# Gating copies of the modulation loads moved from VectorE to GpSimd, and the first feed-forward weight split ordered behind the second norm

## The chip, the core and the metric

One NeuronCore of a Trainium2 chip runs the whole program. TensorE (PE in the rows, PEld for its weight loads), VectorE (DVE), ScalarE (ACT), GpSimd (POOL) and SyncE (SP, which only issues transfers here) each work through a queue of their own in a fixed order and wait for one another by semaphores. The metric is device microseconds of one execution; less is better.

## What is computed

A decoder block over 256 tokens of width 2048: two parallel branches (attention over 8 heads, and a diagonal state-space scan), merged by gates, then a gated feed-forward layer with a short causal convolution. Both sub-layers are normalised and modulated by vectors that a conditioning vector `c` gives through `w_mod`. What matters here is the second half:

```
mod = silu(c) @ w_mod + b_mod
sh1, sc1, g1, sh2, sc2, g2 = split(mod, 6)
...
merged = sigmoid(gate_a) * (y_attn @ w_attn_br) + sigmoid(gate_s) * (y_ssm @ w_ssm_br)
x  = x + g1 * (merged @ w_out)
h2 = rms_norm(x, norm2_g) * (1 + sc2) + sh2
up = causal_dwconv(h2 @ w_up, conv_w, conv_b)
val, gt = split(up, 2)
x  = x + g2 * ((silu(gt) * val) @ w_down)
```

## The kernel before

All weights are float32 and are streamed once, in pieces of 128 x 1024 (512 KB), through a ring of five buffers named `raw`. A piece is split in two: ScalarE rounds it to a high part `whi` (L186), VectorE subtracts that from the piece to get the low part `wlo` (L191). TensorE then multiplies with both parts (L302, L304 for most stages, L268 to L272 for the first feed-forward block). `whi` and `wlo` have three buffers each, so the splits run two to three pieces ahead of TensorE. A `raw` buffer is free again when its piece has been split.

The stages follow each other as `glup` (the gate of the scan branch), `ppp` (its output projection), `outp` (`w_out`), the second norm, then pairs of `gp` and `vp` (the two halves of `w_up`) and `dp` (`w_down`).

Modulation weights come in between. From the stage `glup` on they have a ring of their own, four buffers named `mraw`. There are two kinds. For the gates g1 and g2, 64 pieces (`in_w_g_dram`) are each multiplied with `cb`, which is silu(c) on all partitions, and summed along the row by one VectorE instruction (L493, "gate product" below). For the last quarter of sh2, eight pieces (`in_w_m_dram`) are multiplied on TensorE (L456, tile `modp`), copied to `rows` (L463), transposed (`modt`, L478) and reduced on VectorE (L479). These eight stand at the second norm.

All loads of weights are issued by SP in one queue, so a load that waits holds back those behind it. Loads of modulation weights would run far ahead of the work if only a free buffer held them. Line 122 holds them back: ahead of the load it copies one element of the newest `wlo` into the first element of the `mraw` buffer. The load, which writes the same buffer, must wait for the copy, and the copy waits for the split and for the buffer.

The second norm works in these steps. `add_to` (L329) adds the last two rows blocks into `x`. ScalarE squares them (L528). TensorE sums the squares over the partitions (`sqs`, L533). In `norm_rows`, VectorE copies the sums (L547), TensorE adds them up (`pv`, L550), VectorE makes `v` (L551), runs ten tiny instructions for the inverse root (L396 to L400), writes two diagonal tiles `dg` (L558), TensorE spreads these over the partitions (`pr`, L559), and VectorE copies the result to `rb` (L560). `modulate` then needs `rb`: L567 makes `t`, ScalarE makes the high part of `hl` (L571), VectorE the low part (L572). The first `gp` matmul needs the first `hl`.

The instructions of each engine are put in order when the program is built, by a scheduler that follows estimated times and may move an instruction ahead of others that stand before it in the code. So the first three splits of `w_up` may land among the steps of the norm, although the code makes them behind it.

GpSimd has little to do from the stage `glup` on: it issues the load of `cb` (L505) and four loads of `x` (L1220).

Of the kernel before, what the change touches and what calls it, by code (L numbers as in the profile page):

```python
# [10 lines left out]
F32 = mybir.dt.float32  # L11
# [31 lines left out]
def block_kernel(ctx: ExitStack, tc: tile.TileContext, I, out):  # L43
    nc = tc.nc
    V, A, PE, DMA = nc.vector, nc.scalar, nc.tensor, nc.sync
# [15 lines left out]
    def py_tile(shape, name):  # L61
        return ps.tile(shape, F32, name=name, tag="py", bufs=1)
# [20 lines left out]
    def w4(name, shape, dt=F32):  # L83
        if int(np.prod(shape[1:])) > 512:
            return post.tile(list(shape), dt, name=name, tag="w8", bufs=2)
        return sm.tile(list(shape), dt, name=name, tag="w4", bufs=2)
# [17 lines left out]
    loaded = []  # L104
    place = {"load": 0}
# [6 lines left out]
    def ring_of(i):  # L112
        return "mod" if plan[i][0] == "m" and "mod" in ring else "w"

    def load_next():
        kind, src, _ = plan[place["load"]]
        r = ring_of(place["load"])
        held[r] += 1
        raw = ring[r]()

        if r == "mod" and "lo" in place:
            V.tensor_copy(raw[:, 0, 0:1], place["lo"][:, 0, 0:1].bitcast(F32))
        flat = raw.rearrange("p a b -> p (a b)")
        DMA.dma_start(flat, src)
        loaded.append((raw, r))
        place["load"] += 1

    behind = {}

    def after(inst, earlier):  # L130

        tc.add_manual_dep(inst.ins, earlier.ins.name,
                          mybir.DependencyInfo(mybir.DependencyClass.NoSync, mybir.DependencyReason.DATA),
                          reason="order")
# [5 lines left out]
    def unload(i):  # L140
        held[loaded[i][1]] -= 1
        loaded[i] = None

    def load_ahead():
        while place["load"] < len(plan):
            r = ring_of(place["load"])
            if held[r] >= room[r]:
                break
            load_next()

    def load_until(i):
        while place["load"] <= i and place["load"] < len(plan):
            load_next()
# [28 lines left out]
    hi_lo = {}  # L182
# [5 lines left out]

    def split_lo(i):
        lo = wp.tile([128, 2, 512], F32R, name="wlo", tag="wlo", bufs=WB)  # L190
        V.tensor_sub(lo, loaded[i][0], hi_lo[i][0].bitcast(F32))  # L191
        hi_lo[i][1] = lo
        place["lo"] = lo
        unload(i)
# [11 lines left out]
    def split_ahead(n):  # L206
        while done["hi"] <= n + WB - 1 and done["hi"] < len(weights):
            load_until(weights[done["hi"]])
            split_hi(weights[done["hi"]])
            split_lo(weights[done["hi"]])  # L210
            done["hi"] += 1
# [22 lines left out]
    def flush():  # L234
        while agenda:
            clock["step"] = min(agenda)
            for f in agenda.pop(clock["step"]):
                f()
# [156 lines left out]
    def rsqrt(y, v, t):  # L395
        V.tensor_scalar(y.bitcast(I32), v.bitcast(I32), -0.5, 1597463007.0, op0=ALU.mult, op1=ALU.add)  # L396
        for _ in range(3):
            V.scalar_tensor_tensor(t, y, -0.5, y, op0=ALU.mult, op1=ALU.mult)
            V.tensor_mul(t, t, v)
            V.scalar_tensor_tensor(y, t, 1.5, y, op0=ALU.add, op1=ALU.mult)  # L400
# [120 lines left out]
    rb = const.tile([128, 256], F32, name="rb")  # L521
# [19 lines left out]
    def norm_rows(st, after=None):  # L541

        v2 = sm.tile([128, 2], F32, name="v2", tag="v2", bufs=1)
        r2 = sm.tile([128, 2], F32, name="r2", tag="r2", bufs=1)
        t2 = sm.tile([128, 2], F32, name="t2", tag="t2", bufs=1)
        sqs = w4("sqs", (128, 256))
        V.tensor_copy(sqs, st["p"])  # L547
        pv = py_tile([128, 2], "pv")
        for t in range(2):
            PE.matmul(pv[:, t:t + 1], sqs[:, 128 * t:128 * t + 128], ones[:, 0:1], start=True, stop=True)  # L550
        V.tensor_scalar(v2, pv, 1.0 / (32 * D), EPS, op0=ALU.mult, op1=ALU.add)  # L551
        rsqrt(r2, v2, t2)
        pr = py_tile([128, 256], "pr")
        dg = w4("dg", (128, 2, 128))
        if after is not None:
            V.tensor_copy(dg[:, 0, 0:1], after)
        for t in range(2):
            V.tensor_scalar(dg[:, t], ident, r2[:, t:t + 1], None, op0=ALU.mult)  # L558
            PE.matmul(pr[:, 128 * t:128 * t + 128], ones, dg[:, t], start=True, stop=True)  # L559
        V.tensor_copy(rb, pr)  # L560

    def modulate(c, src, a, sh):

# [455 lines left out]
    for q in range(8):  # L1019
        squares(st1, range(2 * q, 2 * q + 2), xT[q])  # L1020
    norm_rows(st1, a1[:, 0:1])
    mods += m0[len(m0) // 2:]
    all_mods()
# [217 lines left out]
    st2 = {}  # L1241
# [11 lines left out]
    all_mods()  # L1253
    go()
    flush()
    norm_rows(st2)
    mods += late
    all_mods()
    go()
# [149 lines left out]
```

## Time and profile before

| | |
|---|---|
| median of three runs | 1552.86 us (1548.08 to 1556.23) |
| the profiled execution's own time | 1551.37 us |
| its span, first to last instruction | 1549.6 us |
| PE busy in the span | 1491.3 us (96%) |
| VectorE busy | 1052.7 us (68%) |
| ScalarE busy | 847.4 us (55%) |
| GpSimd busy | 11.3 us (1%), 25 instructions |
| mean granted TensorE clock | 0.992 |
| bytes moved | 354.54 MB, 229 GB/s on average |

Line numbers are those of the kernel before. An interval in brackets in a row is the idle time of that engine just ahead of the instruction, with what ended it by the profile. The rows of matmuls overlap each other, since they are pipelined. All times within the execution count from the start of the span.

### The profile page before, as it was taken

To read this page: it belongs to the slowest core of one execution; us is meant where nothing else is said; L and a number is where in the kernel's file an instruction comes from. 1 tells how busy PE (TensorE), PEld (TensorE's weight loads), DVE (VectorE), ACT (ScalarE), POOL (GpSimd) and SP (SyncE) were. 2 spreads that over 40 slices of the span, in tenths; PEclk is the share of its full clock that TensorE was granted. 3 is DMA by queue.
4 is the path that set the end of the run, shared out by engine and by line. 5 is a ranking of instruction groups with operands and counts; after the bars stand their busy time and mean duration, and the time that the engine had idled before them with its cause. 6 is when DMAs were issued, how large, how long until landed. Compare 5 with 4: busy or idle time off the path is not lost.

```text
span 1549.6 us, 24718 instructions
## 1 busy us (share of the span) xinstructions
PE 1491.3 (96%) x9624; PEld 1239.2 (80%) x9624; DVE 1052.7 (68%) x1778; ACT 847.4 (55%) x1201; POOL 11.3 (1%) x25
## 2 busy tenths in 40 slices
PE   6999989999999999899989999999999999999998
PEld 3656757689886678788869888888888888888887
DVE  2787443786774567799769888887555576666654
ACT  3766656967674543654435555555444455555442
POOL 1000000000000000000000000000000000000000
PEclk9999999999999999999999999999999999999999
DMA  8887777643348776879877777776555555565663
GB/s 308 282 311 279 251 269 255 233 166 121 124 150 284 276 251 209 294 255 345 309 254 241 247 247 257 243 252 207 190 191 190 190 187 190 191 189 189 203 210 111
DMA packets 99252, 354.54 MB, mean 229 GB/s; under 512 B 10976, under 2 KB 13152, under 8 KB 99008
## 3 DMA queue, kind: packets, MB, share of 16 engines
q1 hardware_dynamic: 97808, 348.17, 65.5%
q0 software_dynamic: 1184, 4.66, 0.8%
q8 instruction: 75, 1.23, 0.3%
q14 instruction: 41, 0.34, 0.1%
q10 hardware_dynamic: 144, 0.14, 0.0%
HBM read 350.83 MB, written 2.10 MB: 228 GB/s over the span
## 4 chain that ended last, share of the span: by engine, by line
PE 78%; DVE 8%; DMA 8%; ACT 5%; issue 2%; SPq 0%; ACTq 0%; DVEq 0%; POOLq 0%
PE vp L302 10%; PE dp L302 10%; PE gp L302 10%; PE dp L304 5%; PE vp L304 5%; PE gp L304 5%; DMA raw<-in_w_in_dram 3%; PE outp L302 3%; DVE wlo L191 3%; PE modp L456 3%; PE gap L302 3%; ACT whi L186 2%; PE ppp L302 2%; PE outp L304 2%; PE gap L304 2%
## 5 line engine op out<-in xcount | busy, mean ns | idle before, releaser
L191 DVE TENSOR_TENSOR wlo<-raw,whi 128x1024 fp32r<-128x1024 f32 x464 | 566.8, 1224 | 404.4 <-ACT whi L186 401.9
L186 ACT CAST whi<-raw 128x1024 fp32r<-128x1024 f32 x464 | 486.7, 1050 | 562.3 <-PE dp L302 131.9
L302 PE MATMUL vp<-hl,whi 128*128 128x512 f32 x704 | 247.2, 395 | 0.5 <-DVE gate L1272 0.5
L302 PE MATMUL dp<-g,whi 128*128 128x512 f32 x704 | 244.5, 391 | 0.0
L302 PE MATMUL gp<-hl,whi 128*128 128x512 f32 x640 | 224.5, 395 | 0.0
L304 PE MATMUL dp<-g,wlo 128*128 128x256 f32 x704 | 197.8, 281 | 0.0
L304 PE MATMUL vp<-hl,wlo 128*128 128x256 f32 x704 | 197.4, 280 | 0.0
L304 PE MATMUL gp<-hl,wlo 128*128 128x256 f32 x640 | 179.5, 280 | 0.0
L302 PEld LDWEIGHTS vp<-hl,whi 128*128 128x128 f32 x704 | 132.0, 188 | 31.8 <-issue 0.8
L302 PEld LDWEIGHTS dp<-g,whi 128*128 128x128 f32 x704 | 131.9, 187 | 28.7
L302 PEld LDWEIGHTS gp<-hl,whi 128*128 128x128 f32 x640 | 120.0, 187 | 28.1
L304 PEld LDWEIGHTS dp<-g,wlo 128*128 128x128 f32 x704 | 133.0, 189 | 0.0
L304 PEld LDWEIGHTS vp<-hl,wlo 128*128 128x128 f32 x704 | 133.0, 189 | 0.0
L304 PEld LDWEIGHTS gp<-hl,wlo 128*128 128x128 f32 x640 | 120.9, 189 | 0.0
L302 PE MATMUL gap<-hl,whi 128*128 128x512 f32 x256 | 93.9, 406 | 0.6 <-ACT whi L186 0.5
L302 PE MATMUL outp<-m,whi 128*128 128x512 f32 x256 | 91.2, 400 | 0.2 <-DVE m L1155 0.2
L493 DVE SCALAR_TENSOR_TENSOR mraw<-mraw,cb 128x1024 f32<-128x1024 f32 x64 | 77.8, 1220 | 16.1 <-DMA mraw<-in_w_g_dram 9.2
L456 PE MATMUL modp<-raw,cpad 128*32 128x512 f32 (+1 forms) x544 | 75.2, 561 | 6.0 <-DMA raw<-in_w_m_dram 3.6
L304 PE MATMUL gap<-hl,wlo 128*128 128x256 f32 x256 | 72.9, 285 | 1.1 <-DVE wlo L191 0.9
L304 PE MATMUL outp<-m,wlo 128*128 128x256 f32 x256 | 71.7, 281 | 0.2 <-DVE wlo L191 0.2
L302 PEld LDWEIGHTS gap<-hl,whi 128*128 128x128 f32 x256 | 48.1, 188 | 20.6 <-ACT whi L186 4.2
L302 PEld LDWEIGHTS outp<-m,whi 128*128 128x128 f32 x256 | 48.0, 188 | 14.4 <-issue 2.5
(339 smaller groups left out, 2554.5 us busy)
## 6 DMA issues: line engine op xcount, KB each, us to landing
raw<-in_w_up_dram SPq DMA_DIRECT2D x176, 512.0 KB, 4.3
raw<-in_w_m_dram SPq DMA_DIRECT2D x120, 512.0 KB, 5.2
raw<-in_w_in_dram SPq DMA_DIRECT2D x96, 512.0 KB, 4.8
raw<-in_w_down_dram SPq DMA_DIRECT2D x88, 512.0 KB, 3.5
mraw<-in_w_g_dram SPq DMA_DIRECT2D x64, 512.0 KB, 5.0
raw<-in_w_ga_dram SPq DMA_DIRECT2D x32, 512.0 KB, 3.9
raw<-in_w_out_dram SPq DMA_DIRECT2D x32, 512.0 KB, 5.6
raw<-in_w_attn_br_dram SPq DMA_DIRECT2D x16, 512.0 KB, 4.8
```

The costliest lines, as they stand in the source:

```text
L186: A.copy(hi, loaded[i][0])
L191: V.tensor_sub(lo, loaded[i][0], hi_lo[i][0].bitcast(F32))
L302: follow(PE.matmul(joined(p[m]), hi4[:, k, ms], joined(a), start=u == 0 and k == 0, stop=False, skip_group_check=True))
L304: PE.matmul(p[m][:, 0], lo4[:, k, ms], a[:, 0], start=False, stop=u == kbs - 1 and k == 3, skip_group_check=True)
L456: mm = PE.matmul(st["p"][r0:r0 + 32], cpad[:, k], raw[:, i], start=k < 4, stop=k >= 12, tile_position=(0, r0))
L493: V.scalar_tensor_tensor(flat, flat, 1.0, cb[:, 1024 * half:1024 * half + 1024], op0=ALU.mult, op1=ALU.mult, accum_out=sums[:, k, half:hal ...
```

## The change

The copy of line 122 is issued on GpSimd in place of VectorE. It copies the same element, and the load waits for it as before. `norm_rows` hands back its last instruction, the copy to `rb`, and the first `wlo` split that the code makes after the second norm may not stand ahead of that copy on VectorE. This is an order only, without a semaphore.

```
@@ load_next
         if r == "mod" and "lo" in place:
-            V.tensor_copy(raw[:, 0, 0:1], place["lo"][:, 0, 0:1].bitcast(F32))
+            nc.gpsimd.tensor_copy(raw[:, 0, 0:1], place["lo"][:, 0, 0:1].bitcast(F32))
@@ split_lo
-        V.tensor_sub(lo, loaded[i][0], hi_lo[i][0].bitcast(F32))
+        split = V.tensor_sub(lo, loaded[i][0], hi_lo[i][0].bitcast(F32))
+        if "norm" in behind:
+            after(split, behind.pop("norm"))
@@ norm_rows
-        V.tensor_copy(rb, pr)
+        return V.tensor_copy(rb, pr)
@@ behind the stage outp
-    norm_rows(st2)
+    behind["norm"] = norm_rows(st2)
```

The scheduler's order changes with it, on VectorE, TensorE, ScalarE and SP, and only between the stage `glup` and the end of the gate products. In the changed kernel the line numbers behind the second edit are two higher. Three places follow.

VectorE at the start of the second norm, in the kernel before (`v` and `r` are the steps of the inverse root):

```order
L547 COPY sqs<-sqs 128x256
L122 COPY mraw<-wlo 128x1 x2
L551 TENSOR_SCALAR v_7874<-pv 128x2
L122 COPY mraw<-wlo 128x1 x2
L396 TENSOR_SCALAR r_7875<-v_7874 128x2
L191 TENSOR_TENSOR wlo<-raw,whi 128x1024
L398 SCALAR_TENSOR_TENSOR t_7876<-r_7875 128x2
```

The same place in the changed kernel:

```order
L549 COPY sqs<-sqs 128x256
L553 TENSOR_SCALAR v_7874<-pv 128x2
L398 TENSOR_SCALAR r_7875<-v_7874 128x2
L400 SCALAR_TENSOR_TENSOR t_7876<-r_7875 128x2
L401 TENSOR_TENSOR t_7876<-t_7876,v_7874 128x2
```

The four copies and the split between the steps are gone. The end of the same norm on VectorE, before:

```order
L558 TENSOR_SCALAR dg<-p_73,r_7875 128x128 x2
L560 COPY rb<-pr 128x256
L122 COPY mraw<-wlo 128x1 x2
L567 SCALAR_TENSOR_TENSOR t<-x_6697,a_103,rb 128x256 x3
L572 SCALAR_TENSOR_TENSOR hl<-t,sh_102,hl 128x256 x2
```

And in the changed kernel:

```order
L560 TENSOR_SCALAR dg<-p_73,r_7875 128x128 x2
L562 COPY rb<-pr 128x256
L191 TENSOR_TENSOR wlo<-raw,whi 128x1024 x3
L569 SCALAR_TENSOR_TENSOR t<-x_6697,a_103,rb 128x256 x3
L574 SCALAR_TENSOR_TENSOR hl<-t,sh_102,hl 128x256
```

Two copies have left, and three splits now stand between `rb` and the first `t`: the one shown above, and two that stood ahead of the last `add_to` before. TensorE through the norm, before:

```order
L533 MATMUL sqs<-sq,ones 32x256 x2
L456 MATMUL modp<-mraw,cpad 32x512 x4
L550 MATMUL pv<-ones,sqs 128x1 x2
L456 MATMUL modp<-mraw,cpad 32x512 x4
L559 MATMUL pr<-dg,ones 128x128 x2
L456 MATMUL modp<-mraw,cpad 32x512 x7
L268 MATMUL gp<-hl,whi 128x256
```

And in the changed kernel:

```order
L458 MATMUL modp<-mraw,cpad 32x512 x4
L552 MATMUL pv<-ones,sqs 128x1 x2
L458 MATMUL modp<-mraw,cpad 32x512 x3
L561 MATMUL pr<-dg,ones 128x128 x2
L458 MATMUL modp<-mraw,cpad 32x512 x8
L270 MATMUL gp<-hl,whi 128x256
L480 MATMUL modt<-p_73,rows 128x128 x4
```

One `modp` product, the first of the fifth piece, has moved from ahead of `pr` to behind it, and the transposes `modt` now follow the first `gp` matmul, where six stood ahead of them before. The last place is VectorE late in the stage `outp`, where pieces 21 to 23 of `w_out` are split, before:

```order
L191 TENSOR_TENSOR wlo<-raw,whi 128x1024
L493 SCALAR_TENSOR_TENSOR mraw,gsum<-mraw,cb 128x1024
L122 COPY mraw<-wlo 128x1
L493 SCALAR_TENSOR_TENSOR mraw,gsum<-mraw,cb 128x1024
L191 TENSOR_TENSOR wlo<-raw,whi 128x1024
L319 TENSOR_TENSOR ts<-ts,outp 128x512
L493 SCALAR_TENSOR_TENSOR mraw,gsum<-mraw,cb 128x1024
L329 SCALAR_TENSOR_TENSOR x_7099<-ts,g_104,x_7099 128x256
L191 TENSOR_TENSOR wlo<-raw,whi 128x1024
```

And in the changed kernel:

```order
L191 TENSOR_TENSOR wlo<-raw,whi 128x1024
L495 SCALAR_TENSOR_TENSOR mraw,gsum<-mraw,cb 128x1024 x3
L321 TENSOR_TENSOR ts<-ts,outp 128x512
L331 SCALAR_TENSOR_TENSOR x_7099<-ts,g_104,x_7099 128x256
L191 TENSOR_TENSOR wlo<-raw,whi 128x1024
```

The third gate product, the addition L319 and one `add_to` have moved from behind the middle split to ahead of it. On SP the load of that product has moved likewise, from behind the load of the middle piece to ahead of it. At the start of the stage `glup`, SP issues the eighth piece of `w_glu` ahead of the first gate loads; before, four gate loads stood ahead of it. On GpSimd nine copies stand ahead of the first two loads of `x`, seven ahead of the third, one ahead of the fourth, and 55 behind.

## Rows read from the trace of the kernel before

**Rows 1.** The page: busy time of each engine, its share and instructions.
```profile
PE 1491.3 (96%) x9624; PEld 1239.2 (80%) x9624; DVE 1052.7 (68%) x1778; ACT 847.4 (55%) x1201; POOL 11.3 (1%) x25
```

**Rows 2.** Windows: length, busy PE, PEld, DVE, ACT, POOL; clock; DMA share, GB/s.
```profile
653.00:700.00 47.00, 46.24 (x266) 40.38 (x265) 46.38 (x71) 26.14 (x34) 1.43 (x2) 1.00 0.76 266
700.00:763.00 63.00, 62.66 (x354) 51.80 (x354) 56.98 (x102) 26.82 (x32) 1.42 (x2) 1.00 0.90 340
792.00:808.00 16.00, 12.08 (x61) 5.89 (x62) 10.15 (x39) 4.42 (x10) 0.00 (x0) 0.79 0.72 262
808.00:1060.00 252.00, 251.50 (x1482) 220.86 (x1481) 211.32 (x338) 141.40 (x182) 0.00 (x0) 1.00 0.73 248
```

**Rows 3.** Waits of PE from 612 to 1060: us in total, times, longest.
```profile
PE glup L302 <- DVE ts L319: 4.6, 1, 4.6
```

**Rows 4.** Line 122: all its copies, ns each (least, median, most).
```profile
L122 DVE COPY mraw<-wlo x72: 143/147/155, 621.4 to 1048.1; 128x1 f32<-128x1 f32 x72
```

**Rows 5.** Timeline of DVE in the second norm: start, us, instruction, idle before.
```profile
796.30 0.23 DVE L122 COPY mraw<-wlo 128x1 f32<-128x1 f32 x2 [0.82 <-PE modp L456]
...
796.57 1.23 DVE L191 TENSOR_TENSOR wlo<-raw,whi 128x1024 fp32r<-128x1024 f32 x1
797.71 0.15 DVE L398 SCALAR_TENSOR_TENSOR t<-r 128x2 f32<-128x2 f32 x1
...
799.54 0.48 DVE L558 TENSOR_SCALAR dg<-p,r 128x128 f32<-128x128 f32 x2
801.21 0.42 DVE L560 COPY rb<-pr 128x256 f32<-128x256 f32 x1 [1.18 <-PE pr L559]
803.05 0.23 DVE L122 COPY mraw<-wlo 128x1 f32<-128x1 f32 x2 [1.42 <-PE modp L456]
803.20 1.27 DVE L567 SCALAR_TENSOR_TENSOR t<-x,a,rb 128x256 f32<-128x256 f32 x3
```

**Rows 6.** Timeline of PE in the same stretch.
```profile
798.07 1.02 PE L456 MATMUL modp<-mraw,cpad 128*32 128x512 f32 x2 [1.79 <-DVE t L399]
799.97 1.20 PE L559 MATMUL pr<-dg,ones 128*128 128x128 f32 x4 [0.89 <-DVE dg L558]
801.10 3.69 PE L456 MATMUL modp<-mraw,cpad 128*32 128x512 f32 x14
804.72 0.58 PE L268 MATMUL gp<-hl,whi 128*128 128x256 f32 x1
```

**Rows 7.** Windows, PE alone: length, busy, granted clock, DMA share, GB/s.
```profile
799.70:806.20 6.50, 6.23 (x24) 0.50 0.63 240
```

**Rows 8.** DMA issues from 796.85 to 797.00: KB, us from issue to landing.
```profile
mraw<-in_w_m_dram SPq DMA_DIRECT2D x1, 512.0 KB, 5.9
```

**Rows 9.** Chain that ended last, 612 to 640: start, us, what.
```profile
620.86 7.71 DMA cb<-in_c_dram
...
635.45 0.61 DVE ts L319
```

**Rows 10.** Timeline of DVE late in the stage outp.
```profile
755.14 1.22 DVE L493 SCALAR_TENSOR_TENSOR mraw<-mraw,cb 128x1024 f32<-128x1024 f32 x1
...
756.57 1.23 DVE L191 TENSOR_TENSOR wlo<-raw,whi 128x1024 fp32r<-128x1024 f32 x1 [0.21 <-ACT whi L186]
757.71 0.68 DVE L319 TENSOR_TENSOR ts<-ts,outp 128x512 f32<-128x512 f32 x1
758.31 1.22 DVE L493 SCALAR_TENSOR_TENSOR mraw<-mraw,cb 128x1024 f32<-128x1024 f32 x1
```

**Rows 11.** Timeline of PE: first matmul with that split, and with the next.
```profile
757.85 0.39 PE L304 MATMUL outp<-m,wlo 128*128 128x256 f32 x1
...
761.13 0.39 PE L304 MATMUL outp<-m,wlo 128*128 128x256 f32 x1 [0.19 <-DVE wlo L191]
```

**Rows 12.** Waits of ACT from 700 to 792.
```profile
ACT whi L186 <- DMA raw<-in_w_out_dram: 16.0, 8, 4.4
```

**Rows 13.** Timeline of POOL: its only work on one element a partition.
```profile
0.25 0.09 POOL L1398 MEMSET const-float32-0.0<- 128x1 f32 x1 [0.25 <-issue]
```

## The prediction

> **What bounds the kernel now.** I read the page first: TensorE is busy 96% of the span, VectorE 68% [rows 1]. So I looked for the stretches in which TensorE is not full, by the windows, and then for what ends its idle time there. Line 122 runs only between 621 and 1048 us [rows 4], and the norm lies at 792 to 808, so nothing outside 612 to 1060 changes. From 808 to 1060 TensorE is busy 251.50 of 252.00 us, from 653 to 700 all but 0.76, from 700 to 763 all but 0.34 [rows 2]. What can be won is therefore in two places. One is the second norm: 16 us with 3.92 us idle and a mean clock of 0.79 [rows 2], because the granted clock is at 0.50, the lower of its two levels (1.2 against 2.4 GHz), for 6.5 us [rows 7], behind 1.79 and 0.89 us of idle time [rows 6]. The other is one wait of 4.6 us in the stage glup [rows 3]. A chance to lose lies late in the stage outp, where the first matmul with a low part starts 0.05 us behind the end of its split [rows 10, 11] and where eight high-part casts waited for a load [rows 12].
>
> **The copies leave VectorE.** There are 72 of 0.147 us [rows 4], or 10.6 us of VectorE time. TensorE hides them: its whole idle time in the three long windows is 0.76 + 0.34 + 0.50 = 1.6 us [rows 2], which is the most they can give back outside the norm and glup. I take 0, since what is idle there is not named after a copy. Bounds 0 and -1.6 us.
>
> **The chain of the norm on VectorE.** With `v` made, VectorE sat idle 0.82 us until 796.30, because the copies waited for TensorE to free a buffer; then came two copies and the split at 796.57, and the inverse root went on at 797.71 [rows 5]. Without these it starts at 796.30 - 0.82 = 795.48, one step of about 0.2 us comes first, and the step of 797.71 comes at 795.7: 2.0 us earlier. `dg` moves from 799.54 to 797.54. `pr` followed `dg` by 0.43 us [rows 5, 6]; it also stood behind the product of the fifth piece, which occupied 798.07 to 799.09 [rows 6] and would have held it; since that product now stands behind `pr`, it follows at 797.97. With its 1.20 us [rows 6], `rb` is ready at 801.63 - 2.0 = 799.63.
>
> Then the three splits come. They are pitched 1.14 us (796.57 to 797.71 [rows 5]), so 3.4 us, and the first `t` starts at 803.05, against 803.20 [rows 5]. Before, the same gap held two copies and 1.42 us of waiting [rows 5], and two of the three splits had been done for nothing in VectorE's idle time ahead of the norm. So of the 2.0 us, 0.15 is left; 0.6 more if `pr` runs at the full clock and takes half its time. That is what hides the gain: work put back where it is in the way.
>
> TensorE has a bound of its own there. The last `modp` piece is issued at about 796.9 and lands 5.9 us later, at 802.8 [rows 8]; its buffer comes free by TensorE itself, so no copy on any engine makes it earlier. The products of the last pieces run from 801.10 to 804.79, and the first `gp` follows at 804.72 [rows 6]. With less of a backlog the last piece, about 1 us of work at this clock (two rows took 1.02 us [rows 6]), could end near 804.0: 0.7 us at most to win. Against that, `rows` and the four `modt` now come behind the first `gp` matmul rather than the sixth, and the copy to `rows` stands ahead of the second `hl` on ScalarE, so a late last piece holds more. Together I take -0.3 us, with bounds of -0.7 and +1.0. The raw buffers of the delayed splits come free later too, so the sixth piece of `w_up` is loaded behind the norm; five lie ready by then, one for each step, and I cost that at nothing.
>
> **The order in the stage outp.** VectorE ran a gate product at 755.14, the split of the 22nd piece at 756.57, then the addition (0.60 to the next start), then another product (1.14) and an `add_to` [rows 10]. Now the third product, the addition and one `add_to` stand ahead of the split: 755.14 + 2 x 1.14 + 0.60 + 0.40 = 758.4, so the split ends at 759.65 instead of 757.80. TensorE, which used it at 757.85 [rows 11], would be 1.85 us late. The next step waited 0.19 us for its own split [rows 11], which is not lost twice: 1.66. The other end is 0, if the gate loads there land early enough for the products to run in VectorE's gaps. I take +1.4, near the upper end, because the order is fixed and VectorE is busy 56.98 of 63 us there [rows 2].
>
> **The stage glup.** The wait of 4.6 us ends a chain that starts with the load of `cb`, 7.71 us from 620.86 [rows 9]. Four gate loads shared the DMA engines with it. They now stand behind one more weight load and come about 1 us later. Half of that as a gain for `cb` gives -0.5 us; bounds 0 and -1.1. The copies there are queued behind the issue of `cb` on GpSimd, which is not waited for.
>
> **The copies arrive on GpSimd.** No row shows such a copy. The nearest is a fill of one element, 0.09 us [rows 13]; on VectorE the copy took 0.147 [rows 4]. With one more hop between engines I take 0.2 us a load; the lower end is 0, the upper a whole VectorE instruction of 1.23 us [rows 5] to be waited out. SP waits for the copy, and weight loads stand behind it in SP's queue. From 808 on TensorE is full and the loads run ahead. In the stage outp eight casts waited for loads [rows 12]: 8 x 0.2 = 1.6 us at most, and nearly all of it fits in the steps between; I take +0.2. The four loads of `x` stand behind copies that came earlier in time than they did, so 0.
>
> Sum: 0 - 0.3 + 1.4 - 0.5 + 0.2 = +0.8 us. Against the profiled execution's own 1551.37 us that is 1552.2. That execution lies 1.5 us under the median of the runs, 1552.86, to which the forecast refers: **1553.7 us**.
>
> **Rivals.** First, *the clock stays up*. With `pr` 2 us earlier TensorE's idle time splits into shorter pieces, and the fall to 0.50 may not come. The lower level over 6.5 us [rows 7] costs at most half of that, 3.25 us, part of which only replaces waiting for the loads. For it speaks the earlier `pr`; against it that the fifth to eighth pieces still trickle in until 802.8. It gives -3.25 - 0.8 = about -4: 1549 us. Chance 0.12.
>
> Second, *the clock stays down longer*. TensorE now stands idle between the last `modp` and the first `hl`, behind three splits, where before it was busy without a gap from 799.97 on [rows 6]. A second stretch as long would cost 3.25 us: 1557 us. Chance 0.12.
>
> Third, on the other side, *each copy on GpSimd waits out a VectorE instruction*. A copy becomes ready when a split ends, and VectorE goes on at once with another instruction of 1.2 us. If that keeps GpSimd from its data, each modulation load comes 1.0 us later than I took, and the weight loads behind it on SP with it. Eight casts had no slack: 8 x 1.0 us, and the last `modp` piece 1.0 more, is +9, with the +0.8 near 1562 us. It decides from about 0.9 us a copy. For it speaks only that outp has no slack; against it that the waits there were not TensorE's yet. Chance 0.08.
>
> The Trainium skill speaks for this third case: its page "SBUF — State Buffer", section "Who interferes with whom", says that a VectorE instruction with two inputs in SBUF (the split is one) and a GpSimd instruction that reads SBUF exclude each other, and that the second to start is blocked for the whole of the first. By that rule the sum would be near +9, without it +0.8. The trace before cannot show it, since no GpSimd instruction there reads SBUF.
>
> That the change moves nothing is excluded by the order: the copies and the splits have moved.
>
> **How the numbers follow.** The forecast has 0.68. A measurement of this kernel can tell about 0.5%, 7.8 us, from no change. The forecast and the first two rivals lie within that; the third lies just beyond it. Faster 0.03 (the clock case with all bounds at their low ends), same 0.89, slower 0.08. The range: the low bounds add up to -1.6 - 0.7 - 1.1 = -3.4 and the first rival to -4, the high ones to 1.0 + 1.66 + 1.6 = +4.3 and the second rival to +4; single runs scatter by 4 us to either side, a median by less. 1548 to 1560.
>
> **What would show it.** In the profile after: `t` near 803.05 - 792 = 11 us behind the start of the norm as before, with three splits ahead of it; `pr` two microseconds closer to `pv`; the last `modp` landing unchanged; a TensorE wait for a low part near 1.5 us late in outp, where 0.2 was; the wait in glup near 4.1. A clock of 0.50 for less than 3 us or more than 9 shows the first or the second rival. GpSimd copies that start more than 0.5 us behind their split, with SP waiting for them, show the third. I am wrong in kind if TensorE's idle time in the norm falls below 2 us, or if new waits appear past 808.

## The result: half a per cent slower, and a loss at a place that the forecast had called full

Over 22 runs each the kernel after takes 1555.63 us (1548.72 to 1563.4), the kernel before 1548.42 us (1539.58 to 1556.23). The ratio is **1.0051, 95% interval 1.0035 to 1.0067**: some 8 us slower. The forecast, 1553.7 us in 1548 to 1560, holds the time. But it gave a change of +0.8 us, and one of its own signs of being wrong in kind has come: new waits of TensorE past 808 us. Here and below, ratios leave out single executions in a slower state, such as one of 1812.76 us.

The profiled execution of after is the shortest of its 22 runs, and its span, 1546.9 us, is even 2.7 us below that of before. That can't be read as a gain. In front of the stage glup, where the two programs do the same, this execution is already 6.8 us ahead. The first matmul of glup, on the timeline of TensorE (start, us, instruction), of before and of after:

```profile
620.06 0.39 PE L302 MATMUL glup<-y,whi 128*128 128x512 f32 x1
```

```profile
613.28 0.39 PE L304 MATMUL glup<-y,whi 128*128 128x512 f32 x1
```

From there to the end of the span before takes 1549.6 - 620.1 = 929.5 us and after 1546.9 - 613.3 = 933.6 us: +4.1 us even in this good execution. The comparison has to be made stage by stage. (Past the change, line numbers of after are 2 higher.) The windows of after, put 6 us earlier for this head start, with the columns of [rows 2]:

```profile
694.00:757.00 63.00, 61.92 (x353) 51.56 (x352) 56.54 (x85) 28.28 (x32) 11.91 (x18) 1.00 0.88 333
786.00:802.00 16.00, 11.82 (x68) 5.48 (x67) 11.61 (x34) 4.00 (x9) 2.44 (x7) 1.00 0.69 251
802.00:1054.00 252.00, 246.78 (x1455) 216.21 (x1454) 204.44 (x303) 138.82 (x181) 18.02 (x29) 1.00 0.70 244
```

The last window is the loss: TensorE idle for 5.22 of 252 us, where it had been idle for 0.50 [rows 2]. GpSimd, which had nothing there, is now busy 18.02 us with 29 copies. What TensorE waited for from 606 to 1054 us (us in total, times, longest):

```profile
PE glup L304 <- DVE ts L321: 4.4, 1, 4.4
PE gp L306 <- DVE wlo L191: 4.4, 3, 2.5
...
PE outp L306 <- DVE wlo L191: 1.1, 1, 1.1
```

The second row is new: three times a matmul with a low part of the feed-forward stage waits for its split on VectorE. And VectorE's own waits in the feed-forward window, before (808 to 1060 us) and then after (802 to 1054 us):

```profile
DVE mraw L493 <- DMA mraw<-in_w_g_dram: 7.8, 10, 2.1
```

```profile
DVE mraw L495 <- DMA mraw<-in_w_g_dram: 28.8, 16, 3.9
```

So the chain is: a gate load lands late, the gate product (line 495) holds VectorE until it does, the split queued behind the product is late, and TensorE waits for that split. The copies themselves, all 72 (on VectorE: [rows 4]), and those of the feed-forward window (count, busy us, mean ns):

```profile
L122 POOL COPY mraw<-wlo x72: 178/306/2253, 614.6 to 1048.3; 128x1 f32<-128x1 f32 x72
```

```profile
L122 POOL COPY mraw<-wlo 128x1 f32<-128x1 f32 x29 | 18.0, 621 | 232.8 <-DVE wlo L191 228.5 <-DVE g L499 4.3
```

One such copy took 143 to 155 ns on VectorE [rows 4]; on GpSimd it takes 178 to 2253. Which ones are long is seen by setting GpSimd's timeline beside VectorE's. GpSimd (start, us, instruction, idle before):

```profile
1002.21 2.18 POOL L122 COPY mraw<-wlo 128x1 f32<-128x1 f32 x1 [10.02 <-DVE wlo L191]
1010.61 0.19 POOL L122 COPY mraw<-wlo 128x1 f32<-128x1 f32 x1 [6.22 <-DVE wlo L191]
1017.97 1.05 POOL L122 COPY mraw<-wlo 128x1 f32<-128x1 f32 x1 [7.17 <-DVE wlo L191]
1028.67 1.05 POOL L122 COPY mraw<-wlo 128x1 f32<-128x1 f32 x1 [9.64 <-DVE wlo L191]
1039.90 2.25 POOL L122 COPY mraw<-wlo 128x1 f32<-128x1 f32 x1 [10.18 <-DVE wlo L191]
```

VectorE:

```profile
1010.40 0.68 DVE L321 TENSOR_TENSOR ts<-ts,gp 128x512 f32<-128x512 f32 x1
...
1027.32 2.35 DVE L191 TENSOR_TENSOR wlo<-raw,whi 128x1024 fp32r<-128x1024 f32 x2
1029.59 0.69 DVE L1157 TENSOR_TENSOR g<-val,g 128x512 fp32r<-128x512 f32 x1
...
1035.82 1.23 DVE L495 SCALAR_TENSOR_TENSOR mraw<-mraw,cb 128x1024 f32<-128x1024 f32 x1 [3.81 <-DMA mraw<-in_w_g_dram]
...
1038.55 1.22 DVE L191 TENSOR_TENSOR wlo<-raw,whi 128x1024 fp32r<-128x1024 f32 x1
1039.69 0.68 DVE L1293 TENSOR_TENSOR val<-val,gate 128x512 f32<-128x512 f32 x1
1040.29 1.22 DVE L191 TENSOR_TENSOR wlo<-raw,whi 128x1024 fp32r<-128x1024 f32 x1
1041.43 0.68 DVE L1157 TENSOR_TENSOR g<-val,g 128x512 fp32r<-128x512 f32 x1
1042.06 1.23 DVE L191 TENSOR_TENSOR wlo<-raw,whi 128x1024 fp32r<-128x1024 f32 x1
```

TensorE, at the end of this stretch:

```profile
1039.83 0.39 PE L306 MATMUL gp<-hl,wlo 128*128 128x256 f32 x1 [2.49 <-DVE wlo L191]
```

The chain that ended last, through the same place (start, us, what):

```profile
1027.40 1.15 DVE wlo L191
1028.67 1.06 POOL mraw L122
1029.74 5.98 DMA mraw<-in_w_g_dram
1035.82 1.23 DVE mraw L495 x2
...
1038.63 1.15 DVE wlo L191
1039.83 0.39 PE gp L306
```

This is a loop that closes on itself: split, copy, load, gate product, split. Two splits run back to back from 1027.32 until 1029.67. The copy hangs on the first, starts at 1028.67 and is done only at 1029.72, with the end of the second. The load follows at 1029.74. VectorE has nothing else to do from 1032.01 on, for 3.81 us; the gate product starts at 1035.82, the split behind it at 1038.55, and TensorE, which needed that split, has lost 2.49 us at 1039.83. The copies of 1002.21 and 1039.90 last over two and three VectorE instructions in a row (the one of 1039.90 until 1042.15; `g<-val,g` ends at 1042.11). The copy of 1010.61 ran beside `ts<-ts,gp`, whose second input lies in TensorE's accumulators (`gp` is what TensorE writes), and took 0.19 us.

This is what the Trainium skill says on its page "SBUF — State Buffer", section "Who interferes with whom": a VectorE instruction with two inputs in SBUF and a GpSimd instruction that reads SBUF exclude each other. The trace agrees, 1.05 us against 0.19; what it adds is that the copy was not always let in between two such instructions: it was not at the seams within the copies of 1002.21 and 1039.90, but it was at 1029.72, where `g<-val,g` follows the split, and at 1042.15, where a split follows `g<-val,g`.

A second thing had moved with the copies. Without them in its queue, VectorE's order puts three gate products of this stage one split earlier: the 47th stands behind 239 splits instead of 240, the 58th behind 271 instead of 272, the 62nd behind 283 instead of 284. In the profile of after TensorE's three long waits are for the 272nd, the 281st and the 284th split. The first and the last of these stand directly behind such a product; the one of 1035.82 above is the 62nd. The middle one (1.13 us) stands behind the 61st, which has not moved; its load had been held by the copy of 1017.97.

What had not come with the change is that these loads start late. The same place in the kernel before, on VectorE and, last, on SP:

```profile
1030.94 2.45 DVE L191 TENSOR_TENSOR wlo<-raw,whi 128x1024 fp32r<-128x1024 f32 x2
...
1033.91 0.15 DVE L122 COPY mraw<-wlo 128x1 f32<-128x1 f32 x1
...
1037.77 1.23 DVE L191 TENSOR_TENSOR wlo<-raw,whi 128x1024 fp32r<-128x1024 f32 x1 [1.00 <-ACT whi L186]
...
1040.55 1.21 DVE L493 SCALAR_TENSOR_TENSOR mraw<-mraw,cb 128x1024 f32<-128x1024 f32 x1
```

```profile
1034.08 0.33 SPq L124 DMA_DIRECT2D mraw<-in_w_g_dram  x1
```

The first of the two splits ends at 1030.94 + 1.22 = 1032.16; the copy, 0.15 us long, waits in VectorE's queue behind the second split and `g`, and the load starts 1.9 us behind the first split. After the change it starts at 1029.74, 1.2 us behind the split that ended at 1028.55. It is the same at the 47th and the 58th product (1.9 us before, 1.2 to 1.3 after). So at the three products that moved, the loads start earlier behind their split than before, for all the length of GpSimd's copies. What changed for the worse is that the product, before, stood behind the 284th split, which did not have to wait for it. GpSimd's longest copies, of 2.2 us, held the loads of the 48th, 59th and 63rd product, which have not moved (2.3 to 2.4 us behind their split, 1.7 before); no wait of TensorE stands right behind these.

### The profile page after: what moved, and what is told of

It reads as the page before. It is cut to its first block, busy times and chain, and to the rows that moved or that the text cites. A ratio compares the mean times of both kernels' runs of the same rounds, so it can differ in the third digit from the quotient of the medians.

```text
span 1546.9 us, 24827 instructions
## 1 busy us (share of the span) xinstructions
PE 1489.4 (96%) x9624; PEld 1236.6 (80%) x9624; DVE 1046.4 (68%) x1706; ACT 846.6 (55%) x1201; POOL 49.5 (3%) x97
## 4 chain that ended last, share of the span: by engine, by line
PE 68%; DMA 9%; DVE 8%; ACT 4%; issue 2%; POOL 0%; SPq 0%; ACTq 0%; DVEq 0%; POOLq 0%
PE dp L304 10%; PE vp L304 10%; PE gp L304 9%; PE dp L306 5%; PE vp L306 5%; PE gp L306 5%; DVE wlo L191 3%; DMA raw<-in_w_in_dram 3%; PE gap L304 2%; PE outp L304 2%; PE ppp L304 2%; ACT whi L186 2%; PE modp L458 2%; DMA mraw<-in_w_g_dram 2%; DMA raw<-in_w_ga_dram 1%
```

## The experiments

Ratios below are to the kernel before, which was run again beside each group (medians of 1546.3 to 1549.0 us), with 95% intervals; 12 runs each unless said.

**First: which part, and which stage?** Theory: the copies on GpSimd, in the feed-forward stage. Rivals: the edge behind the norm, or the copies in the output projection, where the forecast had put its losses.

The edge alone, the copies back on VectorE:

```diff
-            nc.gpsimd.tensor_copy(raw[:, 0, 0:1], place["lo"][:, 0, 0:1].bitcast(F32))
+            V.tensor_copy(raw[:, 0, 0:1], place["lo"][:, 0, 0:1].bitcast(F32))
```

> Only the edge that puts the first feed-forward split behind the copy into rb; the one-element copies stay on VectorE. Theory (the loss comes from the copies on GpSimd in the feed-forward stage, where a late gate load holds VectorE and the splits behind it): within 0.3% of the kernel before, or down to 4 us faster if the clock also stays up in the norm; no wait of TensorE for a low part after the norm. Rival (three splits behind rb cost the loss): 7 to 8 us slower than before, as the whole change.

Measured: 1547.04 us, 0.9990 (0.9966 to 1.0014). The loss isn't the edge's.

The copies alone, without the edge:

```diff
-    behind["norm"] = norm_rows(st2)
+    norm_rows(st2)
```

> Only the copies moved to GpSimd; no edge behind the norm. Theory: 6 to 10 us slower than before, with 3 to 6 us of waits of TensorE for low parts between 808 and 1060 us and more than 20 us of VectorE's waits for gate loads there (7.8 before). Rival (the edge costs it): within 2 us of the kernel before.

Measured: 1552.65 us, 1.0030 (1.0011 to 1.0050): slower, less than expected. In its profile VectorE waits 34.2 us for gate loads from 808 on, and TensorE 5.6 us for splits there.

The copies on one engine up to the norm, and on another from there on:

```diff
-            nc.gpsimd.tensor_copy(raw[:, 0, 0:1], place["lo"][:, 0, 0:1].bitcast(F32))
+            place["by"].tensor_copy(raw[:, 0, 0:1], place["lo"][:, 0, 0:1].bitcast(F32))
...
     mods += late
     all_mods()
     go()
+    place["by"] = V
```

(with `place["by"]` set to `nc.gpsimd` at the start; in the second kernel the two are exchanged.)

> The whole change, but the copies go back to VectorE once the norm has been issued: GpSimd copies for the loads of the stages glup, ppp, outp and norm only. Theory: the loss is gone, within 2 us of the kernel before, and VectorE's waits for gate loads from 808 on are back under 12 us. Rival (GpSimd's copies cost it in the output projection, where splits end 0.1 us ahead of their use): 5 to 8 us slower than before.

> The reverse: copies on VectorE up to the norm, with the edge behind the norm, and on GpSimd for the 28 or so gate loads of the feed-forward stage. Theory: the whole loss, 6 to 10 us slower than before, with TensorE's waits for low parts at the splits behind the gate products of 1000 to 1040 us. Rival (the output projection): within 2 us of the kernel before.

Measured: GpSimd first, 1547.36 us, 0.9991 (0.9971 to 1.0012); GpSimd in the feed-forward stage, 1555.47 us, **1.0045** (1.0026 to 1.0064). So the last 32 copies, on GpSimd for the feed-forward stage, cost the loss, and the 40 ahead of them nothing that can be measured. The profile of the second one also shows what a wait can bring with it. Its longest wait (2.2 us) ends at 1010.8; in the window from 1008 (columns as above) the mean granted clock is 0.79, so part of it ran at the lower level:

```profile
PE gp L306 <- DVE wlo L191: 3.8, 3, 2.2
```

```profile
1008.00:1016.00 8.00, 5.81 (x25) 4.74 (x24) 5.02 (x9) 2.48 (x3) 2.19 (x1) 0.79 0.44 143
```

Three other profiles show the same behind their longest wait: the copies alone (2.5 us, then a mean clock of 0.57 from 1008 to 1012), the run below with each copy made twice (2.7 us, 0.57 from 1011 to 1015) and the one with the exact places (2.3 us, 0.59 from 1042 to 1046). The profiled execution of after had no such fall behind its 2.49 us. Its mean clock over the whole run is 0.996, and those of the 22 runs lie between 0.987 and 0.996 (the profile of before has 0.992), so most of them had more falls than this one, here or elsewhere. That fits a median further from before (+7.2 us) than this profile (+4.1); so do the two paces of TensorE described at the end.

**Second: the long copies, or the early places of the products?** The change moved both, so each was undone or made alone. Undone places, with GpSimd's copies in the feed-forward stage (an order edge only, for products counted from 0; `splits` and `products` list these instructions as the code makes them):

```diff
+    put = {35: 209, 46: 239, 57: 271, 61: 283}
...
-            V.scalar_tensor_tensor(flat, flat, 1.0, cb[...
+            prod = V.scalar_tensor_tensor(flat, flat, 1.0, cb[...
+            if len(products) in put:
+                after(prod, splits[put[len(products)]])
```

> As the run with GpSimd copies in the feed-forward stage only, but four gate products (the 36th, 47th, 58th and 62nd) are held one split later on VectorE, where they stood before the change; GpSimd's copies stay. If the places of the products cost the loss: back to within 2 us of the kernel before (1547 to 1551), TensorE's waits for low parts gone. If the length of GpSimd's copies costs it (0.6 us on average against 0.15): still 4 to 7 us slower than before.

Measured: 1549.0 us, 1.0018 (0.9994 to 1.0043). The edge for the 36th product moved nothing; the other three stood one split later again. The waits for low parts are gone, the loss shrinks and can't be told from none; nor, with an interval up to 1.0043, from most of the 0.45% above. At the three products the loads still start 1.2 us behind their split. GpSimd's other copies became shorter too, without an edit of theirs, since VectorE's rows around them changed: no copy is over 1.05 us.

```profile
L122 POOL COPY mraw<-wlo x32: 185/308/1051, 800.8 to 1045.1; 128x1 f32<-128x1 f32 x32
```

Early places, with the copies on VectorE:

```diff
-                after(prod, splits[put[len(products)]])
+                after(splits[put[len(products)]], prod)
```

> As the run with the norm's edge alone (copies on VectorE), but the splits are held behind the same four products, so that these stand one split earlier, as after the change. If the places cost the loss: 4 to 8 us slower than before, with waits of TensorE for low parts between 1000 and 1045 us. If the copies' length costs it: within 2 us of the kernel before.

Measured: 1551.81 us, 1.0040 (1.0015 to 1.0066). Its profiled execution, with a span of 1545.3 us below that median, shows only 1.0 us of waits behind the splits of `gp`. Since the edges had pushed three other products one split later, a further run added edges for these, so that every gate product of the stage stands behind as many splits as after the change, with the copies still on VectorE:

> Copies on VectorE, the norm's edge, and the gate products of the feed-forward stage held at exactly the places that they have after the change (the run with four of them moved had pushed three others one split later). If an early place alone costs the loss: 0.3 to 0.6% slower. If it takes GpSimd's long copies too: within 0.2% of the kernel before.

Measured (11 runs): 1553.87 us, **1.0044** (1.0023 to 1.0064), with the waits:

```profile
PE gp L309 <- DVE wlo L193: 2.6, 2, 2.3
PE vp L309 <- DVE wlo L193: 1.3, 2, 1.0
```

So early products lose time even with short copies. That was the half of the theory that I had not expected. A copy on VectorE is short, but it stands in VectorE's queue: in this trace the loads of the 58th and the 62nd product start 1.8 us after the end of the split that they hang on, 0.15 us of it the copy. With the edge alone they start as late, 1.8 us, and nothing is lost, for there the products stand one split later. So the loss needs the early places, and it does not need GpSimd's long copies.

Each of GpSimd's copies made twice, with the early places:

```diff
             place["by"].tensor_copy(raw[:, 0, 0:1], place["lo"][:, 0, 0:1].bitcast(F32))
+            if place["by"] is not V:
+                place["by"].tensor_copy(raw[:, 0, 0:1], place["lo"][:, 0, 0:1].bitcast(F32))
```

> As the run with GpSimd copies in the feed-forward stage only, but each of these copies is made twice, so that a load waits for two. If the copies' length costs the loss: another 4 to 8 us on top of that run's 6.5 (1559 to 1563). If the places cost it: 1554 to 1557, as that run.

Measured (7 runs): 1557.07 us, 1.0083 (1.0052 to 1.0115), an interval that still overlaps the one with single copies (1.0026 to 1.0064); TensorE's waits of `gp` for splits grow from 3.8 to 6.6 us:

```profile
PE gp L308 <- DVE wlo L193: 6.6, 4, 2.7
```

That points to the delay of a load as the other part. A late load alone costs nothing (the edge alone); the question left was whether early places alone would do.

**Third: early places without the delay.** No copy at all. The load's DMA depends on the split. In the trace, from 820 us on, SP does not wait at such a load itself, and each is issued 0.4 us after the end of its split: the weight load ahead of it in SP's queue has already waited.

```diff
-            nc.gpsimd.tensor_copy(raw[:, 0, 0:1], place["lo"][:, 0, 0:1].bitcast(F32))
...
-        DMA.dma_start(flat, src)
+        load = DMA.dma_start(flat, src)
+        if r == "mod" and splits:
+            tc.add_manual_dep(load.ins, splits[-1].ins.name,
+                              mybir.DependencyInfo(mybir.DependencyClass.Sync, mybir.DependencyReason.DATA),
+                              reason="hold back")
```

> The whole change without any copy: each modulation load's DMA depends on the last split directly, so nothing runs on GpSimd, while the gate products of the feed-forward stage keep the places on VectorE that they have after the change. If the copies' length costs the loss: within 2 us of the kernel before or faster. If the places cost it: 4 to 8 us slower than before.

Measured: 1546.97 us, 1.0006 (0.9984 to 1.0028); VectorE's waits for gate loads from 808 on are 8.3 us, as before. The cleanest case changes one instruction and leaves every engine's order as it is after the change: a memset, which reads nothing, in place of the copy.

```diff
-            nc.gpsimd.tensor_copy(raw[:, 0, 0:1], place["lo"][:, 0, 0:1].bitcast(F32))
+            mark = nc.gpsimd.memset(raw[:, 0, 0:1], 0.0)
+            tc.add_manual_dep(mark.ins, splits[-1].ins.name,
+                              mybir.DependencyInfo(mybir.DependencyClass.Sync, mybir.DependencyReason.DATA),
+                              reason="hold back")
```

> The whole change, every engine's order unchanged, but GpSimd's one-element operation is a memset that reads nothing and depends on the split directly. If the copies are long because GpSimd and VectorE both read on-chip memory: the operation is under 0.3 us wherever it falls, and the loss shrinks from 0.45 to 0.5% to under 0.25%. If GpSimd is held up whatever it does there: operations of up to 2.2 us as with copies, and the same loss, 0.4 to 0.55%.

Measured: 1546.6 us, **1.0001** (0.9980 to 1.0021). The loss is gone, with the three products in their early places. All 72 memsets take 0.09 to 0.12 us, wherever they fall:

```profile
L123 POOL MEMSET mraw<- x72: 92/98/118, 617.6 to 1041.3; 128x1 f32 x72
```

The place of the 62nd product reads so now, on VectorE, with 0.60 us of waiting where 3.81 stood:

```profile
1029.64 1.23 DVE L500 SCALAR_TENSOR_TENSOR mraw<-mraw,cb 128x1024 f32<-128x1024 f32 x1 [0.60 <-DMA mraw<-in_w_g_dram]
```

A longer memset tells whether the copies' mean delay or their few long ones count. Of 512 elements a partition it takes 0.53 us, nearly the copies' mean in this stage (0.62), but the same each time:

```diff
-            mark = nc.gpsimd.memset(raw[:, 0, 0:1], 0.0)
+            mark = nc.gpsimd.memset(raw.rearrange("p a b -> p (a b)")[:, 0:512], 0.0)
```

> As the run with memsets, but each fills 512 elements a partition instead of one, which took 0.53 us in the kernel before, so that every load starts about 0.9 us behind its split, the mean with GpSimd's copies (0.83), without their few of 2.2 to 2.4 us; the gate products keep the places that they have after the change. If the mean delay costs the loss: 0.3 to 0.55% slower than before. If it is the few long ones at the early products: within 0.2% of the kernel before.

Measured: 1544.84 us, **0.9992** (0.9975 to 1.0009).

```profile
L123 POOL MEMSET mraw<- x72: 514/526/546, 619.5 to 1043.1; 128x512 f32 x72
```

```profile
DVE mraw L500 <- DMA mraw<-in_w_g_dram: 16.7, 17, 2.6
```

Loads start 0.7 us behind their split here (0.9 had been expected), VectorE waits up to 2.6 us for one of them, and TensorE waits for no split. So a steady delay of 0.7 us is covered, and what isn't are the longer ones at the three early products: 1.2 to 1.3 us with GpSimd's copies, 1.8 with VectorE's. A steady delay as long as the mean behind GpSimd's copies (0.83 in the expectation) was not reached. The start is not the whole of it, either: the loads of these three products then took 4.0 to 4.5 us to land in the run without a copy and with either memset, but 4.8 to 6.0 after the change and 5.6 to 6.5 with VectorE's copies at the exact places. For the 62nd the landing behind its split went from 0.45 + 4.5 us with the short memset to 1.2 + 6.0 after the change, and the larger part of that is the time from issue to landing.

Both parts undone together, no copy and the products one split later:

> No copy on any engine, each modulation load depending on the last split directly, the norm's edge kept, and the four gate products held one split later, where they stood before the change. Both parts of the loss are taken away: within 0.2% of the kernel before or up to 0.3% faster, and TensorE's waits for low parts after 808 us gone. If something else in the change costs time: 0.2 to 0.5% slower.

Measured: 1548.6 us, 1.0019 (0.9999 to 1.0038). No wait for a low part past 808 is left, and it is not faster for that. None of the versions beats the kernel before by more than its interval; the edge alone, GpSimd's copies up to the norm alone and the 512-element memset come nearest (0.9990 to 0.9992).

## Why the prediction was right, and where it was wrong

**The time was right by luck, and by a margin for other things.** The sum gave +0.8 us, the runs show +7.2 in the medians and 0.5% in the ratio. The range held it because its upper end was built from bounds in outp and from a clock that stays down, neither of which is where the time went. And the forecast starts from the median of three runs, 1552.86 us; over 22 runs the kernel before lies at 1548.42, 4.4 us lower. From there the same sum gives 1549.2, 6.4 us short of the measured time.

**Wrong: "from 808 on TensorE is full and the loads run ahead".** In the step on GpSimd's copies that sentence priced 29 of them at nothing. It was read from the weight loads. The loads that the copies hold back are gate loads, and these had little room: VectorE already waited for 10 of them in the kernel before (7.8 us, the row shown above), with splits behind. The loss of this stage is some 7 us (0.45%), not 0. The argument had not been carried from TensorE to VectorE's waits from 808 on, because a full TensorE looked like an end to the question.

**Wrong: which moves of the order mattered.** The working followed the order in the norm and in outp. In the feed-forward stage it left out that three gate products had gone ahead of a split. Runs with these places lose 0.44% even with VectorE's copies and nothing with a short operation; so the early place is one half of the cause and the late load the other. Of the two the change brought the early place. The late load was there before it (1.9 us behind its split, 1.2 after), and cost nothing then.

**The third rival was right about the copy and wrong about its cost.** A GpSimd copy does wait out VectorE's instruction, and at times over several; its sum, 1562 us, lies 6 us above the measured median. But it multiplied 1.0 us by casts in outp, which cost nothing (0.9991 with GpSimd there), and it took for granted that a longer copy makes a later load. The copies are longer, 0.62 us on average in the feed-forward stage against 0.15, and the term of 0.2 us a copy was too small by a factor of three; at the three products that lost time the loads still started 0.6 to 0.7 us earlier behind their split than with VectorE's copies. The length of the copy was the wrong quantity, in the sum and in the rival.

**The norm: right.** VectorE and TensorE of after, as [rows 5, 6]:

```profile
793.02 3.48 DVE L191 TENSOR_TENSOR wlo<-raw,whi 128x1024 fp32r<-128x1024 f32 x3
796.43 0.87 DVE L569 SCALAR_TENSOR_TENSOR t<-x,a,rb 128x256 f32<-128x256 f32 x2
```

```profile
788.65 0.61 PE L552 MATMUL pv<-ones,sqs 128*128 128x1 f32 x4
...
791.96 0.68 PE L561 MATMUL pr<-dg,ones 128*128 128x128 f32 x4 [1.72 <-DVE dg L560]
...
797.37 1.05 PE L458 MATMUL modp<-mraw,cpad 128*32 128x512 f32 x4 [0.21 <-DMA mraw<-in_w_m_dram]
798.35 0.39 PE L270 MATMUL gp<-hl,whi 128*128 128x256 f32 x1
```

And `pv` of before, from which both are counted:

```profile
794.68 0.61 PE L550 MATMUL pv<-ones,sqs 128*128 128x1 f32 x4
```

From `pv` to `pr` it is 3.31 us, and was 799.97 - 794.68 = 5.29: the 2.0 us forecast. `pr`'s four matmuls take 0.68 us, a little over half of [rows 6], and `t` comes 7.78 us behind `pv` instead of 8.52: 0.74 earlier, the 0.15 and the 0.6 "if `pr` runs at the full clock". The three splits fill the gap, and the last w_m piece holds TensorE until 797.37. From `pv` to the first `gp` it is 9.70 us instead of 10.04: -0.34, forecast -0.3. In this execution the clock stayed at 1.00 (window from 786 above), which was the first rival; its 4 us did not come, for TensorE waits for the loads at either clock and is idle for 4.18 us in this window, against 3.92 [rows 2]. The edge alone measures 0.9990 (0.9966 to 1.0014), in which -0.3 us lies, and -5.

**Outp: right in sign, not shown in time.** A wait for a low part of about 1.5 us was forecast where 0.2 was; 1.1 came, and TensorE is idle for 1.08 of 63 us (window from 694 above) where it had been for 0.34 [rows 2]. The run with GpSimd there and VectorE behind it is not slower; its interval ends at +0.12%, or 1.9 us, so +1.4 us is neither shown nor excluded.

**Glup: right in sign.** The wait went from 4.6 to 4.4 us; 4.1 was forecast, so 0.2 of the 0.5 us came.

**What stays open.** Why the loads of the three products take 4.7 to 6.8 us to land in the profiles in which they start 1.2 us or more behind their split, and 4.0 to 4.6 in those in which they start within 0.7, was not tested. And the runs fix the early places and the late loads as joint cause, not each product's share, nor what the 61st, which has not moved, adds.

## What to carry to other kernels

An operation that only releases a load does not cost its own length: what counts is how late the load starts and lands at the consumer with the least room, and a short operation in a busy queue can start it later than a long one in an idle queue. Look at what waits for that load, on every engine, even where the main engine is full. Taking instructions out of one engine's queue also moves what is left in it, and here that made the loss: read the new order in every stage that the instruction was in. If a wait has to be made on GpSimd beside a VectorE that works on two inputs in SBUF, let it be an operation that reads nothing, or hang the load on its cause without an operation.

## What the runs showed of the hardware

GpSimd's one-element copy within SBUF, the on-chip memory that holds all tiles but TensorE's accumulators, took 0.18 us when free. Started while VectorE ran an instruction with two inputs in SBUF, it ended only when that one did, after 0.3 to 1.3 us by what was left of it; in three of the 72 cases (2.18, 2.19 and 2.25 us) it was not let in at the next seam between two such instructions, and at most other seams it was. A memset of one element at the same places took 0.09 to 0.12 us in all of 72 cases.

One and the same row of feed-forward matmuls ran at two paces at a granted clock of 1.00. The 1024th and the 1088th matmul of the stage, counted from 0, before, then with the edge alone:

```profile
977.25 0.40 PE L302 MATMUL vp<-hl,whi 128*128 128x512 f32 x1
...
988.55 0.40 PE L302 MATMUL gp<-hl,whi 128*128 128x512 f32 x1
```

```profile
976.06 0.39 PE L304 MATMUL vp<-hl,whi 128*128 128x512 f32 x1
...
987.16 0.39 PE L304 MATMUL gp<-hl,whi 128*128 128x512 f32 x1
```

Sixty-four matmuls take 11.30 us in the one and 11.10 in the other, without a gap in either. The profile of before stays at the slow pace through the stage, the memset's at the fast one, and after changes between them. 0.2 us in each 64 is 4 to 5 us over the 1600 matmuls of the stage. So two single profiles of this kernel can differ by that much without a cause in the program, and a loss of 8 us has to be settled by repeated runs.
